# Delta stage on normed inputs, with its weight rests and masks on VectorE, in a kernel of six layers on one core

## The chip, the core and the metric

One core of a Trainium2 chip runs the whole program. TensorE (PE; its weight loads are PEld), VectorE (DVE), ScalarE (ACT), GpSimd (POOL) and SyncE (SP, which issues most transfers) each work through a queue of their own and meet by semaphores. The metric is the device time of one execution in microseconds; the median of the runs counts.

## What is computed

Six layers over x (512 tokens, 1024 channels), each with an RMS norm ahead and a residual behind: pooling, gated delta rule, latent attention, pooling, a state space layer with a depthwise convolution beside it, and differential attention. The change touches the delta rule's layer and the state space layer's begin:

```python
h = rmsnorm(x, norm_g)                       # x * rsqrt(mean(x*x) + EPS) * g
proj = h @ w_in
qkv, gate, b_raw, a_raw = jnp.split(proj, ...)
qkv = silu(causal_depthwise_conv(qkv, conv_w))        # 4 taps
q, k, v = jnp.split(qkv, [GDN_QK, 2 * GDN_QK], axis=-1)
...
L = strict lower part of (k_beta @ k.T) * decay
sol = solve_triangular(I + L, [v_beta, k_beta * exp(g)])
...
o = rmsnorm(o, norm_g) * silu(gate);  x = x + o @ w_out
```

and of the state space layer `u = glu_v * sigmoid(glu_g)`, then a causal convolution of 31 taps over u. It reads a norm of a norm: x is first scaled by the final norm of the first four layers.

## The kernel before

Activations lie with channels on the 128 partitions and the 512 tokens in the free dimension: x is eight blocks of 128x512. Every projection is done with three fp32r matmuls per 128 channels of the input (`mm3`, L285 to L290): weight and input are each split into a rounded part and a rest. One unit is a 128-column slab of weights, 128x1024: a transfer (L278), a cast `wh` on ScalarE (L281), a subtraction `wl` on the engine that `self.rest` names (L282), and 24 matmuls of 128x512 into one bank of PSUM. `self.rest` is VectorE, but GpSimd during the delta stage from the first head on (`gdn`, L821 to L829) and in the state space layer (`even`, from L1129).

The inputs of a projection are x times the gain, split by `split_scaled` (L264 to L269) into tiles of the group "h", while the stage before still writes x. The norm r (one number per token, in all partitions) comes later, and each unit's result is scaled by it when it leaves PSUM: in place by `scaled_psum` (L500) ahead of a convolution of four taps (ScalarE L550, VectorE three times L555), or into a tile by `scaled` (L495).

The delta stage, `gdn`: a small unit for the gates, eight units of keys (`k_unit`), of which the last four are woven with `k_chain` (for each head a row broadcast L603, the decays L612 and L615, the product of the keys L691, and its scaling L695); then five units for each of the eight heads (`head_units`), woven with the inverse of the triangular matrices (`inverse`: small products L876 and sums L877, then for each of three levels and four heads a mask L908, matmuls L915, a copy L917, matmuls and subtractions L902, L903), with the recurrence over four chunks (`rec`: L746, L769 to L786) and the norm of its output (L804, L805, split L260, L261).

The state space layer begins with `final_begin`: r of the sum of squares, and from it r2, the norm of the normed x (L1117 to L1120). x itself is scaled by the first norm, one block after each of eight units pairs (`final_x`, L1124), the units' results by r2 (L495). From the second pair on, the taps of the long convolution (L1161) are woven in, with accumulators in the bank "a".

The Tile framework takes the program in the order in which it is written and woven, as priorities, and from dependencies and free buffers fixes the order of each engine's queue when the kernel is built. Buffers come from groups of equal tiles and banks:

```python
TAGS = {"h": 16, "y": 36, "t": 8, "c": 6, "sq": 2, "r": 1, "rope": 3}
BANKS = {"mm": 3, "a": 2, "b": 2, "c": 1}
```

Of the kernel before, what the change touches and what calls it, by code (L numbers as in the profile page):

```python
# [14 lines left out]
ALU = mybir.AluOpType  # L15
# [4 lines left out]
P = 128  # L20
# [148 lines left out]

TAGS = {"h": 16, "y": 36, "t": 8, "c": 6, "sq": 2, "r": 1, "rope": 3}  # L170
BANKS = {"mm": 3, "a": 2, "b": 2, "c": 1}
# [24 lines left out]
class Net:  # L196
# [94 lines left out]

    def proj(self, slabs, h, kt, c=P):

        wv = [
            [w[:, : kt * c].rearrange("p (k c) -> p k c", k=kt) for w in self.load_w(s, kt * c)] for s in slabs
        ]
        nk = kt * len(slabs)
        m = min(c, P)
        out = []
        for j in range(max(c // P, 1)):  # L300
            ps = self.ps()
            for k in range(nk):
                hi, lo = wv[k // kt]
                sl = slice(j * m, j * m + m)
                self.mm3(ps[:m], (hi[:, k % kt, sl], lo[:, k % kt, sl]), h[k], k == 0, k == nk - 1)
            out.append(ps)
        return out
# [73 lines left out]
    def prep(self, i, g):  # L381

        return self.split_scaled(self.x[i], g, "h")

# [233 lines left out]

    def gdn(self, gnext):
        nc, a = self.nc, self.a  # L620
        r = self.norm_r()
        conv = lambda ct, u, tag: self.conv4(u, lambda k: self.p("gconv", k * 32 + ct), tag=tag)

        def conv_unit(ct, tag="t"):
            (ps,) = self.proj([a["gdn_in"][ct]], self.h, 8)
            return conv(ct, self.scaled_psum(ps, r), tag)

# [30 lines left out]
        def k_unit(hd):  # L658
            sil[hd] = conv_unit(8 + hd, "y")
            if hd % 4 == 3:  # L660
                self.silus([sil[i] for i in range(hd - 3, hd + 1)])
                for i in range(hd - 3, hd + 1):
                    sil[i] = sil[i][0]
# [43 lines left out]
        def head_units(hd):  # L707
            st = heads[hd] = {}

            items = []  # L710
# [4 lines left out]
            def gate(i):  # L715
                (ps,) = self.proj([a["gdn_in"][32 + hd * 2 + i]], self.h, 8)
                items.append((self.scaled(ps, r, "y"), self.last, {}))
                if i == 0:
                    return
                self.silus(items)  # L720
                st["q"], _, _, st["g0"], st["g1"] = [it[0] for it in items]
                st["v"] = [self.big("y", shape=[P, 2, 256]) for _ in range(2)]
                for k in range(2):
                    pt = self.transpose4(items[1 + k][0], "c")
                    for j in range(2):
                        nc.vector.tensor_tensor(
                            st["v"][j][:, :, k * P : k * P + P],
                            pt[:, j * 256 : j * 256 + 256].rearrange("p (c d) -> p c d", c=2),
                            sk[:, hd, 2 * j : 2 * j + 2].unsqueeze(2).to_broadcast([P, 2, P]), op=ALU.mult,
                        )  # L730
# [89 lines left out]
        recs = recs()  # L820
        self.rest = nc.gpsimd  # L821
        weave(head_units(0), (solve(0), 4), (k_chain(range(4, 8)), 2))
# [5 lines left out]
        early, rest = self.out_units(self.two_slabs("gdn_out"), y, gnext, ["mm"] * 3)  # L828
        self.rest = nc.vector  # L829
        weave(early, (recs, 99))  # L830
# [3 lines left out]
    def inverse(self, grp, mt, xt):  # L834
# [70 lines left out]
        for l in (1, 2, 3):  # L905
            for n, hd in enumerate(hs):
                ml = self.big("c")
                nc.gpsimd.tensor_tensor(  # L908
                    ml.rearrange("p (c d) -> p c d", c=4), mt[hd].rearrange("p (c d) -> p c d", c=4),
# [93 lines left out]
    def mla(self, gnext):  # L1003
# [39 lines left out]
        def units(hp, st):  # L1043
            def v(vg):
                if vg == 0:
                    state["v"] = [self.big("h") for _ in range(4)]
                vN = state["v"]
# [5 lines left out]
            def q(i):  # L1053
                (ps,) = self.proj([a["mla_uq"][hp * 3 + i]], cq, 6)
                t = self.big("t")
                nc.scalar.copy(t, ps)
                st["q"].append(self.stacked(self.rope(t, cos, sin, mask, "t"), "h") if i == 2 else t)

# [12 lines left out]
        def attend(hp, st, vN):  # L1071
            q, k = st["q"], st["k"]
            for i in range(2):
# [4 lines left out]
                for qb in range(NC):  # L1078
# [9 lines left out]
                    if prev is not None:  # L1088
                        self.weighted(*prev)
                    prev = (pr, qb, vh, po, "h")  # L1090
                    yield 1
# [19 lines left out]
    def final_begin(self):  # L1111
# [7 lines left out]
        r2 = self.norm_of(t, "rope")  # L1119
        nc.vector.tensor_tensor(r2, r2, r, op=ALU.mult)  # L1120
        return r, r2

    def final_x(self, i, r):
        self.nc.vector.scalar_tensor_tensor(  # L1124
            self.x[i], self.x[i], self.p("final", i), r, op0=ALU.mult, op1=ALU.mult
        )

    def even(self, gnext):
        nc, a = self.nc, self.a  # L1129
        rf, r = self.final_begin()  # L1130
        self.rest = nc.gpsimd
        W = lambda i: a["ssd_in"][i]
        u = []

        def plain(slab, tag="t"):
            (ps,) = self.proj([slab], self.h, 8)
            return self.scaled(ps, r, tag)
# [3 lines left out]
        def glu(t):  # L1141
            v = plain(W(24 + t), "y")
            z = plain(W(32 + t))
            nc.scalar.activation(z, z, AF.Tanh, scale=0.5)
# [35 lines left out]
        for t in range(8):  # L1180
            glu(t)
            if t:
                bg(8)
            self.final_x(t, rf)
        self.log_exp()
# [307 lines left out]
def body(tc, a, out, poff, coff, layers=LAYERS):  # L1493
    with ExitStack() as ctx:
# [9 lines left out]
        for n, l in enumerate(layers):  # L1504
# [3 lines left out]
            elif l[0] == "g":  # L1508
                net.gdn(g)
            elif l[0] == "m":  # L1510
# [25 lines left out]
```

## Time and profile before

| what | value |
| --- | --- |
| median of 3 runs | 2520.25 us (2518.78 to 2520.77) |
| the profiled execution's own time | 2517.89 us |
| its span, granted TensorE clock | 2516.1 us, 0.993 |
| busy, PE / PEld | 2447.9 / 1978.1 us |
| busy, DVE / ACT / POOL | 1578.2 / 1066.3 / 475.0 us |
| moved by DMA | 204.41 MB |

Busy shares of PE are of overlapping matmuls: a new one starts before the last one ends. What TensorE loses is seen in its idle time and in the granted clock (1.00 is the upper of its two levels, 2.4 GHz; 0.5 is 1.2 GHz). The delta stage lies from about 319 to 861 us, the state space layer from about 1730 us on. Idle time of an engine is put down to the instruction whose semaphore came last.

### The profile page before, as it was taken

What the parts mean: (1) busy time and instruction counts of PE and PEld (TensorE: products, weight loads), DVE (VectorE), ACT (ScalarE), POOL (GpSimd) and SP (SyncE); (2) the same over time, 40 slices, a digit from 0 to 9 for tenths busy, and PEclk for the clock granted to TensorE, in tenths of its full rate; (3) what the DMA queues carried; (4) which work ended last, traced back from release to release, by engine and by line L of the source; (5) the groups of instructions that cost most, each with busy time, mean ns of one, the idle gap of its engine ahead of it and who ended that gap; (6) DMA issues with size and microseconds to landing.
All of it is one profiled execution on the core that took longest, in us unless ns stands there. A gap on an engine that the chain in (4) does not pass through costs nothing.

```text
span 2516.1 us, 30894 instructions
## 1 busy us (share of the span) xinstructions
PE 2447.9 (97%) x11852; PEld 1978.1 (79%) x11852; DVE 1578.2 (63%) x2796; ACT 1066.3 (42%) x1684; POOL 475.0 (19%) x378
## 2 busy tenths in 40 slices
PE   8999999999999999999999999998999998999999
PEld 6888877877877878888878888887877776877777
DVE  6666367576465354356665466635998897468774
ACT  4323354344444343444454333333244555365553
POOL 0121103423320120000000111214344453100000
PEclk9999999999999999999999999999999999999999
DMA  4232324222112322311212323232222211321122
GB/s 155 94 101 92 97 78 140 82 57 86 51 49 70 104 84 92 97 47 61 64 53 76 98 95 101 92 101 84 85 84 68 68 59 59 99 67 60 59 66 78
DMA packets 73460, 204.41 MB, mean 81 GB/s; under 512 B 19904, under 2 KB 20032, under 8 KB 73312
## 3 DMA queue, kind: packets, MB, share of 16 engines
q1 hardware_dynamic: 72816, 200.91, 24.7%
q8 instruction: 94, 1.54, 0.2%
q10 hardware_dynamic: 288, 0.86, 0.1%
q0 software_dynamic: 208, 0.66, 0.1%
q14 instruction: 54, 0.44, 0.1%
HBM read 195.58 MB, written 6.82 MB: 80 GB/s over the span
## 4 chain that ended last, share of the span: by engine, by line
PE 85%; DVE 8%; ACT 3%; issue 2%; POOL 1%; DMA 0%; SPq 0%; ACTq 0%; DVEq 0%; POOLq 0%
PE psmm L288 23%; PE psmm L290 23%; PE psmm L289 23%; PE psc L998 2%; PE psa L1448 1%; PE psa L1082 1%; PE psb L994 1%; DVE psa L1161 1%; PE psb L896 1%; ACT wh L281 1%; PE psc L368 1%; PE psa L915 1%; PE psb L775 1%; POOL wl L282 1%; DVE c L805 1%
## 5 line engine op out<-in xcount | busy, mean ns | idle before, releaser
L281 ACT CAST wh<-wr 128x1024 fp32r<-128x1024 f32 (+3 forms) x366 | 377.0, 1031 | 779.5 <-PE psmm L289 598.4
L288 PE MATMUL psmm<-h,wh 128*128 128x512 f32 x1704 | 682.8, 401 | 15.9 <-ACT wh L281 8.6
L290 PE MATMUL psmm<-h,wl 128*128 128x512 f32 x1704 | 679.4, 399 | 0.0
L289 PE MATMUL psmm<-h,wh 128*128 128x512 f32 x1704 | 678.1, 398 | 0.0
L282 DVE TENSOR_TENSOR wl<-wr,wh 128x1024 fp32r<-128x1024 f32 (+2 forms) x270 | 321.9, 1192 | 189.5 <-ACT wh L281 187.2
L288 PEld LDWEIGHTS psmm<-h,wh 128*128 128x128 f32 x1704 | 321.6, 189 | 91.0 <-issue 16.8
L289 PE MATMUL psmm<-y,wh 128*128 128x512 f32 x976 | 383.4, 393 | 0.0
L288 PE MATMUL psmm<-y,wh 128*128 128x512 f32 x976 | 383.2, 393 | 0.0
L290 PEld LDWEIGHTS psmm<-h,wl 128*128 128x128 f32 x1704 | 321.0, 188 | 78.6 <-issue 11.4
L290 PE MATMUL psmm<-y,wl 128*128 128x512 f32 x976 | 382.2, 392 | 0.0
L289 PEld LDWEIGHTS psmm<-h,wh 128*128 128x128 f32 x1704 | 321.5, 189 | 71.2 <-issue 5.9
L282 POOL TENSOR_TENSOR wl<-wr,wh 128x1024 fp32r<-128x1024 f32 (+1 forms) x96 | 235.5, 2455 | 491.9 <-ACT wh L281 406.4
L354 POOL TENSOR_TENSOR sq<-sq,sq 128x512 f32<-128x512 f32 x36 | 64.5, 1792 | 831.7 <-ACT sq L356 831.7
L289 PEld LDWEIGHTS psmm<-y,wh 128*128 128x128 f32 x976 | 183.4, 188 | 36.9 <-issue 0.7
L288 PEld LDWEIGHTS psmm<-y,wh 128*128 128x128 f32 x976 | 183.4, 188 | 36.6 <-DVE psa L1161 0.2
L290 PEld LDWEIGHTS psmm<-y,wl 128*128 128x128 f32 x976 | 183.4, 188 | 36.6 <-issue 0.2
L1161 DVE SCALAR_TENSOR_TENSOR psa<-y,par,psa 128x506 f32<-128x506 f32 (+28 forms) x232 | 164.5, 730 | 3.9 <-ACT psa L1157 1.6
L483 DVE TENSOR_TENSOR x<-psmm,x 128x512 f32<-128x512 f32 x44 | 30.3, 691 | 140.4 <-PE psmm L290 140.4
L495 DVE TENSOR_TENSOR t<-psmm,r 128x512 f32<-128x512 f32 (+1 forms) x74 | 50.8, 688 | 101.4 <-PE psmm L290 101.3
L983 ACT ACTIVATE c<-psa,smx,qs 128x128 f32<-128x128 f32 (+3 forms) x128 | 78.9, 617 | 82.7 <-DVE smx L981 81.7
L555 DVE SCALAR_TENSOR_TENSOR t<-psmm,par,t 128x509 f32<-128x509 f32 (+2 forms) x120 | 88.7, 741 | 7.5 <-ACT t L550 5.1
L260 ACT CAST y<-c 128x512 fp32r<-128x512 f32 x60 | 37.1, 621 | 98.9 <-POOL c L531 68.9
(359 smaller groups left out, 3322.7 us busy)
## 6 DMA issues: line engine op xcount, KB each, us to landing
wr<-in_pool_in_dram SPq DMA_DIRECT2D x64, 512.0 KB, 3.7
wr<-in_gdn_in_dram SPq DMA_DIRECT2D x48, 512.0 KB, 3.7
wr<-in_ssd_in_dram SPq DMA_DIRECT2D x48, 512.0 KB, 3.7
wr<-in_pool_out_dram SPq DMA_DIRECT2D x32, 512.0 KB, 3.6
wr<-in_mla_in_dram SPq DMA_DIRECT2D x27, 512.0 KB, 3.7
wr<-in_dif_in_dram SPq DMA_DIRECT2D x24, 512.0 KB, 3.7
wr<-in_mla_uq_dram SPq DMA_DIRECT2D x24, 384.0 KB, 3.0
wr<-in_pool_grp_dram SPq DMA_DIRECT2D x16, 512.0 KB, 3.6
```

Of the source, the lines that this page charges most:

```text
L260: nc.scalar.copy(hi, src)
L281: nc.scalar.copy(hi[:, :f], raw[:, :f])
L282: self.rest.tensor_tensor(lo[:, :f], raw[:, :f], hi[:, :f].bitcast(F32), op=ALU.subtract)
L288: nc.tensor.matmul(ps, wh, xh, start=start, stop=False)
L289: nc.tensor.matmul(ps, wh, xl, start=False, stop=False)
L290: nc.tensor.matmul(ps, wl, xh, start=False, stop=stop)
L354: (eng or nc.gpsimd).tensor_tensor(acc[0], acc[0], acc[1], op=ALU.add)
L495: self.last = self.nc.vector.tensor_tensor(t[:n], ps[:n], r[:n], op=ALU.mult)
L555: self.last = nc.vector.scalar_tensor_tensor(t[:, s:], u[:, : S - s], w(k), t[:, s:], op0=ALU.mult, op1=ALU.add)
L983: nc.scalar.activation(pr[:, :n], ps[:, :n], AF.Exp, bias=st[:, 1:2], scale=scale, accum_out=st[:, 2:3])
L998: nc.tensor.matmul(po[:, qb * P : n], vN[kb], pT[:, kb * P : kb * P + P], start=kb == 0, stop=kb == qb)
L1161: nc.vector.scalar_tensor_tensor(out[:, s:], z[:, : S - s], dw(k), acc[:, s:], op0=ALU.mult, op1=ALU.add)
```

## The change

Four things change. The inputs' splits and some other tiles go from the group "h" (16) to the group "y", which has all 52. In `gdn` only the gates' unit and the units 0 to 2 of the keys take the raw inputs and are scaled in PSUM (unit 2 in the bank "a"); behind unit 2 each block of x is multiplied by gain and norm and split anew by `apply_norm` (L452, cast L260, rest L261), and every later unit takes these, so that its result needs no scaling: the taps read PSUM as it is, and the gates' results are copied by ScalarE (L721). `self.rest` stays VectorE in the whole delta stage, and the 24 masks of `inverse` are VectorE's as well. In `even` `self.rest` becomes GpSimd only behind the second pair of units, one unit each of the second and third pair takes the bank "b", and `final_x` waits by a dependency of its own for the last operation of r2.

```diff
-TAGS = {"h": 16, "y": 36, "t": 8, "c": 6, "sq": 2, "r": 1, "rope": 3}
+TAGS = {"y": 52, "t": 8, "c": 6, "sq": 2, "r": 1, "rope": 3}
...
-    def proj(self, slabs, h, kt, c=P):
+    def proj(self, slabs, h, kt, c=P, bank="mm"):
...
-            ps = self.ps()
+            ps = self.ps(bank)
...
-        return self.split_scaled(self.x[i], g, "h")
+        return self.split_scaled(self.x[i], g, "y")
...
-    def gdn(self, gnext):
+    def gdn(self, g, gnext):
...
-        def conv_unit(ct, tag="t"):
-            (ps,) = self.proj([a["gdn_in"][ct]], self.h, 8)
-            return conv(ct, self.scaled_psum(ps, r), tag)
+        def conv_unit(ct, tag="t", bank="mm", raw=False):
+            (ps,) = self.proj([a["gdn_in"][ct]], self.h, 8, bank=bank)
+            return conv(ct, self.scaled_psum(ps, r) if raw else ps, tag)
...
         def k_unit(hd):
-            sil[hd] = conv_unit(8 + hd, "y")
+            sil[hd] = conv_unit(8 + hd, "y", "a" if hd == 2 else "mm", hd < 3)
+            if hd == 2:
+
+                self.h = [self.apply_norm(self.x[i], g(i), r) for i in range(8)]
...
-                items.append((self.scaled(ps, r, "y"), self.last, {}))
+                z = self.big("y")
+                items.append((z, nc.scalar.copy(z, ps), {}))
...
-        self.rest = nc.gpsimd
         weave(head_units(0), (solve(0), 4), (k_chain(range(4, 8)), 2))
...
-        self.rest = nc.vector
         weave(early, (recs, 99))
...
                 ml = self.big("c")
-                nc.gpsimd.tensor_tensor(
+                nc.vector.tensor_tensor(
...
-        nc.vector.tensor_tensor(r2, r2, r, op=ALU.mult)
-        return r, r2
-
-    def final_x(self, i, r):
-        self.nc.vector.scalar_tensor_tensor(
+        return r, r2, nc.vector.tensor_tensor(r2, r2, r, op=ALU.mult)
+
+    def final_x(self, i, r, after):
+
+        op = self.nc.vector.scalar_tensor_tensor(
             self.x[i], self.x[i], self.p("final", i), r, op0=ALU.mult, op1=ALU.mult
         )
+        info = mybir.DependencyInfo(mybir.DependencyClass.Sync, mybir.DependencyReason.DATA)
+        self.tc.add_manual_dep(op.ins, after.ins.name, info, reason="the norm first")
...
-        rf, r = self.final_begin()
-        self.rest = nc.gpsimd
+        rf, r, last_r = self.final_begin()
...
-            v = plain(W(24 + t), "y")
-            z = plain(W(32 + t))
+
+            v = plain(W(24 + t), "y", "b" if t == 2 else "mm")
+            z = plain(W(32 + t), "t", "b" if t == 1 else "mm")
...
             glu(t)
+            if t == 1:
+                self.rest = nc.gpsimd
             if t:
                 bg(8)
-            self.final_x(t, rf)
+            self.final_x(t, rf, last_r)
```

After the change the line numbers of the recurrence are higher by four (L746 becomes L750), those of `inverse` by two. Left out of the diff are MLA's tiles that go from "h" to "y" and the argument g of `gdn`.

The order on VectorE at the end of the keys' unit 2, before. psmm_2549 is that unit's bank, y_2575 its convolution, and wl the rests of the next weights:

```order
L555 SCALAR_TENSOR_TENSOR y_2538<-psmm_2512,par,y_2538 128x511
L500 TENSOR_TENSOR psmm_2549<-psmm_2549,r_2379 128x512
L282 TENSOR_TENSOR wl_2681<-wr_2678,wh_2680 128x1024
L555 SCALAR_TENSOR_TENSOR y_2575<-psmm_2549,par,y_2575 128x509
L555 SCALAR_TENSOR_TENSOR y_2575<-psmm_2549,par,y_2575 128x510
L555 SCALAR_TENSOR_TENSOR y_2575<-psmm_2549,par,y_2575 128x511
L500 TENSOR_TENSOR psmm_2586<-psmm_2586,r_2379 128x512
L282 TENSOR_TENSOR wl_2755<-wr_2752,wh_2754 128x1024
L555 SCALAR_TENSOR_TENSOR y_2612<-psmm_2586,par,y_2612 128x509
L555 SCALAR_TENSOR_TENSOR y_2612<-psmm_2586,par,y_2612 128x510
L555 SCALAR_TENSOR_TENSOR y_2612<-psmm_2586,par,y_2612 128x511
```

And after the change, from the same scaling on (psa_2549 is the same bank; y_2583, y_2589 and so on are the rests of the normed inputs, c_2580 to c_2622 the products ahead of them):

```order
L500 TENSOR_TENSOR psa_2549<-psa_2549,r_2379 128x512
L282 TENSOR_TENSOR wl_2672<-wr_2669,wh_2671 128x1024
L555 SCALAR_TENSOR_TENSOR y_2575<-psa_2549,par,y_2575 128x509
L261 TENSOR_TENSOR y_2583<-c_2580,y_2582 128x512
L555 SCALAR_TENSOR_TENSOR y_2575<-psa_2549,par,y_2575 128x510
L261 TENSOR_TENSOR y_2589<-c_2586,y_2588 128x512
L555 SCALAR_TENSOR_TENSOR y_2575<-psa_2549,par,y_2575 128x511
L261 TENSOR_TENSOR y_2595<-c_2592,y_2594 128x512
L452 SCALAR_TENSOR_TENSOR c_2616<-x_80,par,r_2379 128x512
L261 TENSOR_TENSOR y_2601<-c_2598,y_2600 128x512
L452 SCALAR_TENSOR_TENSOR c_2622<-x_81,par,r_2379 128x512
L261 TENSOR_TENSOR y_2607<-c_2604,y_2606 128x512
```

The scaling of units 3 (psmm_2586) is gone, and six rests of the normed inputs and two more products stand among the taps.

TensorE's order at the second to fourth pair of key products, before (psa_2857 is such a product, psa_2867 a row broadcast, psmm_2891 a head's unit):

```order
L289 MATMUL psmm_2891<-h_1886,wh_2887 128x512
L290 MATMUL psmm_2891<-h_1885,wl_2888 128x512
L288 MATMUL psmm_2891<-h_1953,wh_2887 128x512
L289 MATMUL psmm_2891<-h_1954,wh_2887 128x512
L691 MATMUL psa_2857<-y_2575 128x128 x4
L603 MATMUL psa_2867<-rope_2455,sel 128x512
L290 MATMUL psmm_2891<-h_1953,wl_2888 128x512
L288 MATMUL psmm_2891<-h_2021,wh_2887 128x512
L289 MATMUL psmm_2891<-h_2022,wh_2887 128x512
L290 MATMUL psmm_2891<-h_2021,wl_2888 128x512
L288 MATMUL psmm_2891<-h_2090,wh_2887 128x512
```

And after, at the same product (psa_2900; psmm_2865 is the keys' last unit, psmm_2934 and psmm_3022 are the first head's):

```order
L694 MATMUL psa_2841<-y_2538 128x128 x4
L603 MATMUL psa_2851<-rope_2455,sel 128x512
L289 MATMUL psmm_2865<-y_2625,wh_2861 128x512
L290 MATMUL psmm_2865<-y_2624,wl_2862 128x512
L288 MATMUL psmm_2934<-y_2582,wh_2930 128x512
L289 MATMUL psmm_2934<-y_2583,wh_2930 128x512
L288 MATMUL psmm_3022<-y_2582,wh_3018 128x512
L289 MATMUL psmm_3022<-y_2583,wh_3018 128x512
L694 MATMUL psa_2900<-y_2575 128x128 x4
L603 MATMUL psa_2910<-rope_2455,sel 128x512
L694 MATMUL psa_2918<-y_2659 128x128 x4
L603 MATMUL psa_3129<-rope_2455,sel 128x512
```

Three products and three broadcasts stand close together, with six projection matmuls between them.

VectorE's order at the state space layer's begin, before (rope_13395 becomes r2, c_13393 the norm's square, x_74 to x_81 are the blocks of x):

```order
L1117 TENSOR_TENSOR c_13390<-r_13381 128x512
L1124 SCALAR_TENSOR_TENSOR x_74<-x_74,par,r_13381 128x512
L1118 TENSOR_TENSOR c_13390<-psc_13388,c_13390 128x512
L1124 SCALAR_TENSOR_TENSOR x_75<-x_75,par,r_13381 128x512
L409 TENSOR_SCALAR c_13393<-c_13390 128x512
L1124 SCALAR_TENSOR_TENSOR x_76<-x_76,par,r_13381 128x512
L399 TENSOR_TENSOR c_13393<-c_13393,rope_13395 128x512
L1124 SCALAR_TENSOR_TENSOR x_77<-x_77,par,r_13381 128x512
L400 TENSOR_TENSOR c_13393<-c_13393,rope_13395 128x512
L1124 SCALAR_TENSOR_TENSOR x_78<-x_78,par,r_13381 128x512
L401 SCALAR_TENSOR_TENSOR rope_13395<-c_13393,rope_13395 128x512
L1124 SCALAR_TENSOR_TENSOR x_79<-x_79,par,r_13381 128x512
```

And after, where r2 is rope_13414:

```order
L282 TENSOR_TENSOR wl_13527<-wr_13524,wh_13526 128x1024
L401 SCALAR_TENSOR_TENSOR r_13400<-c_13398,r_13400 128x512
L1119 TENSOR_TENSOR c_13409<-r_13400 128x512
L1120 TENSOR_TENSOR c_13409<-psc_13407,c_13409 128x512
L409 TENSOR_SCALAR c_13412<-c_13409 128x512
L596 MEMSET rope_14103 128x512
L399 TENSOR_TENSOR c_13412<-c_13412,rope_13414 128x512
L400 TENSOR_TENSOR c_13412<-c_13412,rope_13414 128x512
L401 SCALAR_TENSOR_TENSOR rope_13414<-c_13412,rope_13414 128x512
L1122 TENSOR_TENSOR rope_13414<-rope_13414,r_13400 128x512
L495 TENSOR_TENSOR y_13453<-psmm_13428,rope_13414 128x512
L495 TENSOR_TENSOR t_13486<-psmm_13461,rope_13414 128x512
```

The scalings of x (L1124, now L1126) stand behind r2 and the first two results that need it, and a weight rest stands ahead.

## Rows read from the trace of the kernel before

**Rows 1.** Part 1 of the page: busy us, share of the span, instructions.
```profile
PE 2447.9 (97%) x11852; PEld 1978.1 (79%) x11852; DVE 1578.2 (63%) x2796; ACT 1066.3 (42%) x1684; POOL 475.0 (19%) x378
```

**Rows 2.** Busy us by stretch: length, PE, PEld, DVE, ACT, POOL; PEclk, DMA share, GB/s.
```profile
319.00:391.00 72.00, 71.59 (x350) 57.27 (x349) 51.93 (x101) 41.66 (x59) 7.66 (x4) 1.00 0.33 111
391.00:428.00 37.00, 31.64 (x163) 26.44 (x162) 31.19 (x79) 16.09 (x23) 13.80 (x10) 0.95 0.35 103
480.00:620.00 140.00, 131.41 (x651) 103.83 (x650) 93.32 (x167) 65.28 (x97) 40.51 (x22) 1.00 0.26 75
620.00:720.00 100.00, 94.50 (x562) 80.70 (x561) 54.64 (x87) 39.52 (x58) 34.04 (x19) 1.00 0.13 43
720.00:861.00 141.00, 140.39 (x658) 111.92 (x657) 72.72 (x108) 59.18 (x84) 18.76 (x9) 1.00 0.23 75
1719.00:1765.00 46.00, 38.66 (x155) 30.30 (x154) 30.96 (x34) 17.39 (x22) 18.97 (x8) 0.93 0.22 69
1765.00:2085.00 320.00, 308.44 (x1462) 245.26 (x1461) 288.17 (x433) 146.12 (x247) 150.22 (x100) 0.99 0.22 73
```

**Rows 3.** Waits of PE, 319 to 861: us in total, times, longest.
```profile
PE psb L775 <- DVE c L612: 6.5, 4, 1.8
PE psa L603 <- DVE c L612: 4.1, 1, 4.1
PE psb L775 <- DVE q L771: 2.9, 2, 1.7
PE psa L915 <- POOL c L908: 2.2, 2, 1.7
```

**Rows 4.** Timeline of DVE, 486 to 502: start us, us, line, operation [idle before].
```profile
497.62 0.18 DVE L876 TENSOR_TENSOR y<-y,y 128x16 f32<-128x16 f32 x1
...
498.84 2.21 DVE L876 TENSOR_TENSOR y<-y,y 128x25 f32<-128x25 f32 x1
```

**Rows 5.** Timeline of POOL, 484 to 512.
```profile
498.60 2.40 POOL L282 TENSOR_TENSOR wl<-wr,wh 128x1024 fp32r<-128x1024 f32 x1 [6.62 <-ACT wh L281]
```

**Rows 6.** Groups by form, DVE, 319 to 861: busy us, mean ns | idle before.
```profile
L282 DVE TENSOR_TENSOR wl<-wr,wh 128x1024 fp32r<-128x1024 f32 x23 | 28.1, 1222 | 16.5 <-ACT wh L281 16.5
...
L805 DVE TENSOR_TENSOR c<-c,y 128x512 f32<-128x512 f32 x16 | 19.8, 1277 | 0.0
...
L268 DVE SCALAR_TENSOR_TENSOR h<-x,par,h 128x512 fp32r<-128x512 f32 x7 | 5.2, 746 | 0.0
```

**Rows 7.** Groups by form, POOL, 319 to 861.
```profile
L282 POOL TENSOR_TENSOR wl<-wr,wh 128x1024 fp32r<-128x1024 f32 x40 | 95.5, 2389 | 302.5 <-ACT wh L281 228.3 <-DVE ssq L432 55.3 <-PE psmm L290 6.6
L908 POOL TENSOR_TENSOR c<-y,con 128x512 f32<-128x512 f32 x24 | 32.2, 1357 | 12.5 <-PE psb L901 12.5
```

**Rows 8.** Groups by form, ACT, 319 to 861.
```profile
L260 ACT CAST y<-c 128x512 fp32r<-128x512 f32 x16 | 9.8, 622 | 17.2 <-DVE c L805 17.1
```

**Rows 9.** Timeline of DVE, 319 to 349.
```profile
328.57 0.68 DVE L401 SCALAR_TENSOR_TENSOR r<-c,r 128x512 f32<-128x512 f32 x1
...
345.48 0.69 DVE L500 TENSOR_TENSOR psmm<-psmm,r 128x512 f32<-128x512 f32 x1
```

**Rows 10.** Waits of PE, 1719 to 1765.
```profile
PE psmm L288 <- DVE y L495: 5.7, 1, 5.7
PE psc L368 <- DVE sq L363: 1.6, 1, 1.6
```

**Rows 11.** Timeline of DVE, 1730 to 1757.
```profile
1731.76 2.36 DVE L268 SCALAR_TENSOR_TENSOR h<-x,gfa,h 128x512 fp32r<-128x512 f32 x1 [0.83 <-ACT h L267]
...
1740.22 0.69 DVE L1117 TENSOR_TENSOR c<-r 128x512 f32<-128x512 f32 x1
...
1751.84 2.82 DVE L1120 TENSOR_TENSOR rope<-rope,r 128x512 f32<-128x512 f32 x1
```

**Rows 12.** Waits of PE, 1760 to 2110.
```profile
PE psc L1337 <- ACT y L1165: 2.6, 1, 2.6
```

More of the change, by code (lines that the diff above doesn't have):

```diff
@@ L1045, in v @@
                 if vg == 0:
-                    state["v"] = [self.big("h") for _ in range(4)]
+                    state["v"] = [self.big("y") for _ in range(4)]
                 vN = state["v"]
@@ L1056, in q @@
                 nc.scalar.copy(t, ps)
-                st["q"].append(self.stacked(self.rope(t, cos, sin, mask, "t"), "h") if i == 2 else t)
+                st["q"].append(self.stacked(self.rope(t, cos, sin, mask, "t"), "y") if i == 2 else t)
             def k():
@@ L1089, in attend @@
                         self.weighted(*prev)
-                    prev = (pr, qb, vh, po, "h")
+                    prev = (pr, qb, vh, po, "y")
                     yield 1
@@ L1119, in final_begin, with plain @@
         r2 = self.norm_of(t, "rope")
-        nc.vector.tensor_tensor(r2, r2, r, op=ALU.mult)
-        return r, r2
-    def final_x(self, i, r):
-        self.nc.vector.scalar_tensor_tensor(
+        return r, r2, nc.vector.tensor_tensor(r2, r2, r, op=ALU.mult)
+    def final_x(self, i, r, after):
+        op = self.nc.vector.scalar_tensor_tensor(
             self.x[i], self.x[i], self.p("final", i), r, op0=ALU.mult, op1=ALU.mult
         )
+        info = mybir.DependencyInfo(mybir.DependencyClass.Sync, mybir.DependencyReason.DATA)
+        self.tc.add_manual_dep(op.ins, after.ins.name, info, reason="the norm first")
     def even(self, gnext):
         nc, a = self.nc, self.a
-        rf, r = self.final_begin()
-        self.rest = nc.gpsimd
+        rf, r, last_r = self.final_begin()
         W = lambda i: a["ssd_in"][i]
         u = []
-        def plain(slab, tag="t"):
-            (ps,) = self.proj([slab], self.h, 8)
+        def plain(slab, tag="t", bank="mm"):
+            (ps,) = self.proj([slab], self.h, 8, bank=bank)
             return self.scaled(ps, r, tag)
@@ L1508, in body @@
             elif l[0] == "g":
-                net.gdn(g)
+                net.gdn(gains[l], g)
             elif l[0] == "m":
```

## The prediction

> **What bounds the kernel now.** I read the page's busy shares first: TensorE is busy for 97% of the span [rows 1], so the time can only fall where TensorE stands still or runs at its lower clock. Second, the table by stretch for the delta stage (319 to 861 us) and the state space layer's begin [rows 2]: a stretch's length less its PE time is what TensorE lost. From 391 to 428 that is 37.00 - 31.64 = 5.4 us, from 480 to 620 8.6, from 620 to 720 5.5, from 720 to 861 0.6, but from 319 to 391 only 0.4. The layer's begin, 1719 to 1765, loses 46.00 - 38.66 = 7.3, and its granted clock was 0.93, a further 0.07 x 46 = 3.2 us; in 391 to 428 it was 0.95, or 1.9 us. Third, PE's waits in the delta stage [rows 3]: nearly all end on VectorE (L612, L771) or on a GpSimd mask (L908). Fourth, why VectorE was late, from its timeline and GpSimd's [rows 4, 5]: the product L876 of 128x16 took 0.18 us, the next one, of 128x25, 2.21 us, and that one ran beside GpSimd's weight rest (498.60 to 501.00). A VectorE operation with both inputs in SBUF stands still while GpSimd's tensor operation runs. L805 shows it in the mean, 1277 ns for 128x512 where L268 takes 746 [rows 6]. So GpSimd's 40 rests and 24 masks [rows 7] cost VectorE more than their absence would suggest, and the queue behind the blocked operation is late for TensorE.
>
> **What the change does to each engine.** In the delta stage 40 rests go from GpSimd (95.5 us there) to VectorE: 40 x 1.222 = +48.9 us [rows 6, 7]. 24 masks (32.2 us on GpSimd) follow at about 0.69 us each, near L500's 694 ns: +16.5. New are 8 norm products (746 ns, as L268) and 8 subtractions (0.69): +11.5. Gone are 29 scalings at 0.694 (L500) and 16 gate scalings at about the same: -31.2. What stood still beside GpSimd comes back: L805 alone 16 x (1277 - 694) = 9.3 us; with the others I put it at 20. VectorE's sum is about +26 us. In the five stretches of this stage that the rows show it was busy 303.8 of 490 us, 62%, so the sum isn't a bound; where it falls is. ScalarE gains 8 casts and 16 copies, 24 x 0.62 = +15 us [rows 8], on an engine busy for 42 of 72 and 65 of 140 us there [rows 2]; I cost it at nothing but for the one cast in the chain below. TensorE's matmuls are the same, two rows regrouped. SP issues the same weight transfers in the same order. GpSimd's queue loses what stood behind its rests, the masks: that wait goes with them.
>
> **Begin of the delta stage, +3.5 us.** Up to unit 2 of the keys, projections use raw inputs. The norm r is ready at 329.2 [rows 9], and 8 products have to fit behind it, between the taps of units 0 and 1, into VectorE's idle time (20 of 72 us in this stretch). The order of the change puts the first lower part (L261) behind unit 2's scaling, a rest and a tap. That scaling ran at 345.48 to 346.17 [rows 9]; 1.22 + 0.75 + 0.69 later, at 348.8, the first lower part exists, and TensorE has only two matmuls without it: 3.3 us, where nothing was lost before. Units 3 and 4 then run interleaved, six matmuls for each part. Six take 6 x 71.59/350 = 1.2 us by the stretch's mean, and VectorE needs 0.69 + 0.75 for one part and the tap or product beside it: nearly in step, 0.2 more. Bounds: 1.5, if the casts come early and part of unit 2's end hides it; 8, if a rest (1.22) enters twice and the clock falls as after 1750, where it took 3.2.
>
> **First decay products, +5 us.** In the change's order three pairs of key product and row broadcast (L694, L603) stand on TensorE with six projection matmuls between them, where the order before has 7 to 15 between two pairs; the next projection waits for a rest that VectorE does behind the eight decays (L612) and kk products. The nearest row is the wait of L603 for L612, 4.1 us for one [rows 3]; with half a clock stretch 5. Bounds 0 (VectorE, relieved, is early) and 8 (two such waits).
>
> **391 to 428, -6 us.** The 4.1 us wait [rows 3] and the rest of the 5.4 us come from VectorE work held up by GpSimd's rests and a mask. They go, and the 1.9 us of clock: -7.2 at most; a rest on VectorE in the same place gives some back. Bounds -7.2 and 0, for VectorE is busy 31.19 of 37 us here, the fullest place of the stage.
>
> **428 to 861, -7.4 us.** 8.6 + 5.5 + 0.6 = 14.7 us were lost. L908's 2.2 us go with the mask's queue. L775's waits for L612 and L771 [rows 3] stem from blocked operations, except one of four that I can't put down to GpSimd (6.5/4 = 1.6 stay). New: in heads 4, 6 and 7 a rest lands before the query's product (L750 after the change), 1.22 + 0.69 = 1.9 each, 5.7 us, late for the same L775. 14.7 - 1.6 - 5.7 = 7.4. Bounds: -14.7, and +2 if every head gets such a rest (8 x 1.9 + 1.6 - 14.7).
>
> **State space layer's begin, -8.5 us.** L268 (2.36 us, blocked by GpSimd's rest) goes back to 0.74: the wait of 1.6 us [rows 10] goes. The norm's chain from L1117 (1740.22) to the end of L1120 (1754.66) [rows 11] has the final scalings between its steps, and L1120 alone took 2.82 blocked. Without either it is seven operations at 0.69 or less and ScalarE's two at about 0.62, some 6 us, with one rest of 1.22 ahead: r2 at about 1745.5 to 1748. TensorE wanted it at about 1750 (the wait of 5.7 us [rows 10] ended one result behind L1120's end), and two more banks put that off. The 5.7 us wait and 3.2 us of clock go: -10.5. Given back: 4 rests (4.9 us) and the final scalings come later on VectorE, whose last taps of the long convolution end with TensorE waiting 2.6 us [rows 12]. VectorE has 320 - 288.17 = 32 us of idle time before that [rows 2], so I take 2. Bounds -10.5 and -4.
>
> **One group of buffers, +0.5 us** (-1 to +4): no instruction comes or goes; at MLA's end a few splits come later, in a stage that TensorE fills.
>
> **Sum:** 3.5 + 5 - 6 - 7.4 - 8.5 + 0.5 = -12.9 on the profiled execution's 2517.89 us: 2505.0. The median is 2.4 above that execution, so 2507 for the median of the runs.
>
> **A rule against it.** VectorE is at 84% in the fullest stretch [rows 2] and gets more work there. The Trainium skill's page Perfetto Trace Analysis, section Optimizing Scalar/DVE Operations, says that with a saturated VectorE "offloading some work to Scalar (or even GPSIMD) may make sense", and this change goes the other way; by that rule the stage gets slower, as in the slow rival below. The same section adds that moving work between these two might not help since they share a port; the blocked L876 agrees with that half.
>
> **Rivals.**
> - *Cover holds (0.18).* The begin's 8.5 us hide behind work that I counted as late, and the -14.7 bound is nearly reached: -22, 2498. For it: VectorE's relief is at the very products that TensorE waits for. Against: only two matmuls can run without a lower part.
> - *The delta stage gives nothing (0.17).* Its four terms cancel, and only the state space layer's begin remains: -8.5 + 0.5, 2512. For it: the new waits are of the kind of the old.
> - *The long convolution's tail takes it back (0.12),* or buffers in one group make the scheduler lose at MLA's end: the change doesn't do what it says at that layer. Delta -5, layer -2, MLA +4: 2517, no change that can be told.
> - *VectorE becomes the bound (0.11), slower.* The point from which it decides is added work above VectorE's idle time just where TensorE waits: 37 - 31.2 = 5.8 us are idle in 391 to 428, and GpSimd's 13.8 us there are some 7 at VectorE's price (1.222 for 2.389), so it decides unless the unblocked products give back 1.3 or more. Begin +8, products +8, nothing back in 391 to 428, +2 later, less 8 for the layer: +10, 2530.
>
> **How the numbers follow.** The forecast has 0.42. Some 5 us (0.2%) can be told from no change. Faster: 0.42 + 0.18 + most of the second rival, 0.15, gives 0.75. Same: 0.12 + 0.02 = 0.14. Slower 0.11. The range 2495 to 2519 leaves out the slow rival and the far ends of the others, the bounds of the terms in it.
>
> **What would show it.** Right: L876, L805 and L750 lose their 2 us instances; TensorE's gaps in 391 to 428 and in 1719 to 1765 go, with granted clock 1.00; a new gap of some 3 us stands at 345 to 349 ahead of the first L289 of unit 3, waiting for L261, and one at the kk pairs, waiting for L612 or L282. Wrong: no gap at 345 (first term), or gaps of 2 us in every head that end on L282 or L750 (the slow rival), or a wait at the long convolution's end of over 5 us.

## The result and the profile after

The changed kernel takes 2494.52 us in the median (2493.05 to 2495.28) where the kernel before takes 2520.41: the ratio is 0.9897, 95% interval 0.9885 to 0.9909, some 26 us less where 13 were forecast (2507), and just below the range's end of 2495. The profiled execution's span falls by 23.4 us, from 2516.1 to 2492.7; the other 2.5 come from the kernel before, whose profiled execution was that much below its median, while the changed kernel's was at its median.

Where it came from is read from the ends of the stages, by VectorE's first or last addition to x (L483) in each. The first of the delta stage's end comes at 797.4 instead of 810.5: -13.1. The last of MLA's comes at 1717.4 instead of 1730.2, so MLA gave back 0.3. The last of the state space layer's comes at 2164.9 instead of 2188.3: another -10.6 in that layer. The rest is unchanged.

The stretches of the changed kernel (length, PE, PEld, DVE, ACT, POOL, then granted clock, DMA share, GB/s) answer to [rows 2]; the last one is the state space layer's begin, 13 us earlier than before:

```profile
319.00:391.00 72.00, 65.49 (x310) 51.12 (x309) 55.34 (x108) 42.15 (x62) 1.00 (x4) 0.96 0.25 84
391.00:428.00 37.00, 37.00 (x188) 31.32 (x188) 29.24 (x82) 15.96 (x23) 0.66 (x4) 0.98 0.43 129
...
480.00:620.00 140.00, 139.11 (x710) 111.97 (x709) 95.70 (x176) 69.11 (x105) 0.14 (x1) 1.00 0.25 75
620.00:720.00 100.00, 99.64 (x579) 84.32 (x578) 58.96 (x96) 42.43 (x64) 0.00 (x0) 1.00 0.17 53
720.00:861.00 141.00, 140.69 (x654) 113.30 (x653) 70.93 (x102) 61.25 (x87) 11.73 (x7) 1.00 0.25 78
1706.00:1752.00 46.00, 46.00 (x200) 36.97 (x199) 35.35 (x43) 19.69 (x25) 10.95 (x6) 1.00 0.24 81
```

Nothing is idle in 391 to 428 any more, and from 480 to 861 some 1.6 us are, where 14.7 were; but 319 to 391 has lost 72 - 65.49 = 6.5, against 0.4, at a clock of 0.96. The waits of PE in the delta stage (total, times, longest) answer to [rows 3], of which none is left:

```profile
PE psa L694 <- DVE y L698: 3.0, 2, 2.8
PE psmm L288 <- ACT y L260: 2.4, 1, 2.4
...
PE psb L773 <- DVE q L790: 0.5, 1, 0.5
PE psmm L289 <- DVE y L261: 0.4, 1, 0.4
```

And the groups on VectorE (busy, mean ns | idle before) show that these products no longer stand still: L809, the L805 of before, takes 683 ns in place of 1277, and L750, the L746 of before, 686; the longest L878, the L876 of before, takes 0.61 us in place of 2.21. It does 63 rests where it did 23.

```profile
L282 DVE TENSOR_TENSOR wl<-wr,wh 128x1024 fp32r<-128x1024 f32 x63 | 76.9, 1222 | 56.6 <-ACT wh L281 54.9 <-PE psmm L290 1.6
...
L809 DVE TENSOR_TENSOR c<-c,y 128x512 f32<-128x512 f32 x16 | 10.3, 683 | 0.0
...
L750 DVE TENSOR_TENSOR c<-t,c 128x512 f32<-128x512 f32 x8 | 5.5, 686 | 1.4 <-ACT t L339 1.4
```

### The profile page after: what moved, and what is told of

Its sections match the earlier page's. It is cut to its first block, busy times and chain, and to the rows that moved or that the text cites. A ratio compares the mean times of both kernels' runs of the same rounds, so it can differ in the third digit from the quotient of the medians.

```text
span 2492.7 us, 30840 instructions
## 1 busy us (share of the span) xinstructions
PE 2443.6 (98%) x11852; PEld 1976.8 (79%) x11852; DVE 1586.8 (64%) x2835; ACT 1077.4 (43%) x1708; POOL 336.8 (14%) x310
## 4 chain that ended last, share of the span: by engine, by line
PE 84%; DVE 9%; ACT 3%; issue 2%; POOL 1%; DMA 1%; SPq 0%; ACTq 0%; DVEq 0%; POOLq 0%
PE psmm L288 22%; PE psmm L290 22%; PE psmm L289 22%; DVE psa L1165 3%; PE psc L1000 2%; PE psa L1454 1%; PE psa L1084 1%; PE psb L996 1%; PE psb L898 1%; PE psa L917 1%; PE psc L368 1%; ACT wh L281 1%; PE psb L779 1%; PE psb L903 1%; DVE wl L282 1%
## 5 line engine op out<-in xcount | busy, mean ns | idle before, releaser
L288 PE MATMUL psmm<-y,wh 128*128 128x512 f32 x2656 | 1054.1, 397 | 12.7 <-ACT wh L281 8.5
L289 PE MATMUL psmm<-y,wh 128*128 128x512 f32 x2656 | 1053.7, 397 | 0.4 <-DVE y L261 0.4
L290 PE MATMUL psmm<-y,wl 128*128 128x512 f32 x2656 | 1052.7, 396 | 0.0
L288 PEld LDWEIGHTS psmm<-y,wh 128*128 128x128 f32 x2656 | 500.0, 188 | 124.3 <-issue 11.1
L290 PEld LDWEIGHTS psmm<-y,wl 128*128 128x128 f32 x2656 | 500.0, 188 | 113.5 <-issue 11.5
L289 PEld LDWEIGHTS psmm<-y,wh 128*128 128x128 f32 x2656 | 499.9, 188 | 107.2 <-issue 5.9
L282 DVE TENSOR_TENSOR wl<-wr,wh 128x1024 fp32r<-128x1024 f32 (+2 forms) x314 | 375.6, 1197 | 234.4 <-ACT wh L281 230.9
L1165 DVE SCALAR_TENSOR_TENSOR psa<-y,par,psa 128x495 f32<-128x495 f32 (+28 forms) x232 | 164.6, 732 | 2.9 <-ACT psa L1161 0.8
L282 POOL TENSOR_TENSOR wl<-wr,wh 128x1024 fp32r<-128x1024 f32 (+1 forms) x52 | 129.0, 2483 | 182.4 <-ACT wh L281 175.3
L483 DVE TENSOR_TENSOR x<-psmm,x 128x512 f32<-128x512 f32 x44 | 30.3, 691 | 136.6 <-PE psmm L290 136.6
L495 DVE TENSOR_TENSOR t<-psmm,r 128x512 f32<-128x512 f32 (+1 forms) x74 | 50.8, 688 | 101.5 <-PE psmm L290 101.3
L260 ACT CAST y<-c 128x512 fp32r<-128x512 f32 x68 | 41.5, 620 | 92.6 <-POOL c L531 68.6
L1000 PEld LDWEIGHTS psc<-y,y 128*128 128x128 f32 x480 | 63.3, 192 | 21.8 <-ACT y L998 11.0
L1000 PE MATMUL psc<-y,y 128*128 128x128 f32 x480 | 73.4, 284 | 3.4 <-ACT y L998 2.9
L288 PE MATMUL psmm<-wh,y 128*128 128x256 f32 x256 | 74.3, 290 | 0.0
L289 PE MATMUL psmm<-wl,y 128*128 128x256 f32 x256 | 73.7, 288 | 0.0
L290 PE MATMUL psmm<-wh,y 128*128 128x256 f32 x256 | 73.6, 288 | 0.0
```

The source lines that it names most:

```text
L282: self.rest.tensor_tensor(lo[:, :f], raw[:, :f], hi[:, :f].bitcast(F32), op=ALU.subtract)
L288: nc.tensor.matmul(ps, wh, xh, start=start, stop=False)
L289: nc.tensor.matmul(ps, wh, xl, start=False, stop=False)
L290: nc.tensor.matmul(ps, wl, xh, start=False, stop=stop)
L495: self.last = self.nc.vector.tensor_tensor(t[:n], ps[:n], r[:n], op=ALU.mult)
L1000: nc.tensor.matmul(po[:, qb * P : n], vN[kb], pT[:, kb * P : kb * P + P], start=kb == 0, stop=kb == qb)
```

## Experiments

All are edits of the changed kernel, unless another is named, and are compared with the kernel before on the same chip.

**1. Without the normed inputs.** Every unit takes the raw inputs and is scaled in PSUM; rests and masks stay on VectorE.

```diff
-        def conv_unit(ct, tag="t", bank="mm", raw=False):
+        def conv_unit(ct, tag="t", bank="mm", raw=True):
...
-            sil[hd] = conv_unit(8 + hd, "y", "a" if hd == 2 else "mm", hd < 3)
+            sil[hd] = conv_unit(8 + hd, "y", "mm", True)
-            if hd == 2:
-                self.h = [self.apply_norm(self.x[i], g(i), r) for i in range(8)]
...
-                z = self.big("y")
-                items.append((z, nc.scalar.copy(z, ps), {}))
+                items.append((self.scaled(ps, r, "y"), self.last, {}))
```

> The changed kernel with every unit of the delta stage on raw inputs and scaled out of PSUM again; the rests and masks stay on VectorE. Theory 1 (the gain of the heads comes from GpSimd no longer blocking VectorE; the normed inputs only cost at the begin): the gaps at 345 and 386 us go (2.4 + 0.4 + 2.8 us and two half-clock stretches of 1.7 us), the heads keep nearly all of their gain: 2486 to 2496. Theory 2 (the heads gain because units leave PSUM without a scaling; VectorE would be too full with the rests and the scalings): the heads lose again, 2502 to 2512.

2490.69 us, ratio 0.9886 (0.9869 to 0.9902): theory 1. The normed inputs bring nothing where the rests are on VectorE; the interval overlaps that of the whole change, so whether they cost a little can't be told. The wait at 345 is gone with them. The wait for the key products is not, so my reading, that the order of the normed inputs made it, does not hold:

```profile
PE psa L691 <- DVE y L695: 2.8, 1, 2.8
...
PE psa L603 <- DVE c L612: 0.4, 1, 0.4
```

**2. Rests and masks on GpSimd again.**

```diff
         recs = recs()
+        self.rest = nc.gpsimd
...
+        self.rest = nc.vector
         weave(early, (recs, 99))
...
-                nc.vector.tensor_tensor(
+                nc.gpsimd.tensor_tensor(
                     ml.rearrange("p (c d) -> p c d", c=4), mt[hd]...
```

> The changed kernel with the 40 rests and 24 masks of the delta stage on GpSimd again, normed inputs kept. Theory 1: VectorE's products are blocked again, L876 and L805 with 2 us instances, most of the 14 us of idle time between 428 and 861 come back: 2504 to 2512. Theory 2: the heads stay as they are: 2492 to 2498.

2514.63 us, 0.9985 (0.9974 to 0.9996): 0.0088 or 22 us are lost, somewhat more than theory 1 asked for. What is left of the gain, some 4 us, is less than the state space layer's 11 (experiment 3), so the delta stage is some 7 us slower here than in the kernel before. In the profiled execution it ends 10.7 us later (its first L483 at 821.2), but that execution was the longest of ten. So beside GpSimd's rests the normed inputs do cost; the one group of buffers doesn't (experiment 4), and unit 2's bank was not tried apart.

**3. The state space layer as before,** that is, without the diff's lines from `final_begin` on.

> The changed kernel with the state space layer's begin as it was (rests on GpSimd from its first unit, final scalings between the steps of r2, banks of one group). If the 10.6 us that the trace shows there belong to this part alone: 2504 to 2506, with waits of 1.6 and 5.7 us at its begin. If part of it came from the time shift of the stage before: 2498 to 2502.

2504.49 us, 0.9941 (0.9927 to 0.9956): 11 us of the gain are gone, the layer's part alone. Its waits are 1.6 and 5.7 us, as in [rows 10].

**4. One group of buffers alone,** in the kernel before.

> The kernel before with one group of 52 buffers in place of 16 and 36, nothing else. Theory 1 and 2: no change, 2518 to 2522. Rival 3 (the room in the group lets VectorE and ScalarE run ahead, and part of the gain is its): 2505 to 2516.

2519.67 us, 1.0005 (0.9996 to 1.0015): no change.

**5 and 6. Only the rests, or only the masks, on GpSimd,** one edit of the second experiment each.

> The changed kernel with only the 40 rests of the delta stage on GpSimd again; masks on VectorE. If the rests' 95 us of GpSimd work block VectorE's products: most of the 20 us that rests and masks cost together, 2507 to 2513, with waits of L779 for L612 and L775. If the queue of masks behind rests was the larger part: 2498 to 2502.

> The changed kernel with only the 24 masks on GpSimd again; rests on VectorE. The masks' own share is the waits for L908 and L917 (2.2 + 1.3 us) and the splits that stand beside them: 2496 to 2501 by the blocking of VectorE; 2494 to 2496 if masks harm only when they queue behind rests.

The rests: 2515.63 us, 0.9979 (0.9970 to 0.9988), 2.6 us above what I expected and the whole loss of experiment 2. The masks: 2493.62 us, 0.9894 (0.9879 to 0.9908), none. With the masks PE's longest waits are those of the changed kernel (L694 3.0 us in all, L288 2.4). With the rests old waits are back (L779 is the L775 of before), and the wait of 2.8 us for the key products (L694) has gone down to 0.3:

```profile
PE psb L779 <- DVE c L612: 4.3, 3, 1.7
PE psa L603 <- DVE c L612: 3.9, 1, 3.9
PE psb L779 <- DVE q L775: 3.3, 2, 1.7
```

So masks on GpSimd cost nothing where the rests are on VectorE, and no wait of PE ends on one. That they were late in the kernel before (L915 in [rows 3]) because they queued behind rests fits this, but is not shown by itself: beside the rests they added nothing to the loss either.

**7. GpSimd does rests that nobody reads.** The 40 rests stay on VectorE and are done once more on GpSimd, so nothing reads GpSimd's result. Two things are added: GpSimd is busy, and a weight's buffer comes free only when GpSimd has read it too.

```diff
         self.rest.tensor_tensor(lo[:, :f], raw[:, :f], hi[:, :f].bitcast(F32), op=ALU.subtract)
+        if self.idle:
+            d = self.wp.tile([P, 1024], F32, tag="dum", name=f"dum{n}", bufs=1)
+            nc.gpsimd.tensor_tensor(d[:, :f], raw[:, :f], hi[:, :f].bitcast(F32), op=ALU.subtract)
```

> The changed kernel, rests and masks on VectorE, and for each of the 40 rests the same subtraction once more on GpSimd, into a tile that nobody reads (the group has 50 buffers in place of 52 to make room; the result is the same). If VectorE's standing still beside GpSimd is the cause, the loss comes back though nothing waits for GpSimd: 2505 to 2516, with 2 us instances of L750, L809 and L878. If GpSimd's lateness was the cause: 2493 to 2497.

2517.20 us, 0.9990 (0.9980 to 0.9999): 0.0093 or 23 us are lost, as much as with the real rests on GpSimd, and no wait of PE ends on GpSimd. The groups on GpSimd and VectorE and the waits of PE (line numbers are three higher: L812 is L809, L753 is L750, L782 is L779):

```profile
L285 POOL TENSOR_TENSOR dum<-wr,wh 128x1024 f32<-128x1024 f32 x40 | 119.7, 2993 | 330.0 <-ACT wh L281 304.8 <-issue 25.1
```

```profile
L812 DVE TENSOR_TENSOR c<-c,y 128x512 f32<-128x512 f32 x16 | 12.9, 845 | 0.0
...
L753 DVE TENSOR_TENSOR c<-t,c 128x512 f32<-128x512 f32 x8 | 10.5, 1307 | 1.4 <-ACT t L342 1.4
```

```profile
PE psa L697 <- DVE y L701: 8.3, 5, 3.2
...
PE psb L782 <- DVE c L615: 2.0, 1, 2.0
...
PE psb L782 <- DVE q L778: 1.2, 1, 1.2
```

GpSimd's own subtraction is slowed too, 2993 ns against 2389 in [rows 7]: it stands still for VectorE as well. VectorE is busy for 367.0 us with the same 617 operations that take it 340.8 in the changed kernel. PE's waits end on VectorE's scaling of the key products (L701; the 2.8 us that the changed kernel has are among the 8.3), its decays (L615) and the recurrence (L778). The longest, of 3.2 us at 421.76, comes behind a product of 128x64 on VectorE that takes 0.27 us elsewhere and here ends as GpSimd's subtraction does, with no idle time on VectorE from there to the wait's end:

```profile
414.00 2.11 DVE L883 TENSOR_TENSOR y<-y,y 128x64 f32<-128x64 f32 x1
```

```profile
413.57 2.41 POOL L285 TENSOR_TENSOR dum<-wr,wh 128x1024 f32<-128x1024 f32 x1 [3.22 <-ACT wh L281]
```

The buffers are the rival: weight transfers wait 41.6 us in all for the unread subtractions, and casts 13.1 us for transfers in place of 3.4. But of PE's waits only 0.4 us end on a weight's rest and none on a weight's cast. Another 4.0 us have no releaser in the profile. So VectorE's standing still beside GpSimd brings the loss back without GpSimd's result being late for anything.

**8. Two more operations ahead of the query's product.** They tell whether a delay of the prediction's size harms there.

```diff
+            d = self.small([P, 512], "dum", 1)
+            for _ in range(2):
+                nc.vector.tensor_tensor(d, q, qe, op=ALU.mult)
             nc.vector.tensor_tensor(qe, q, qe, op=ALU.mult)
```

> The changed kernel with two more products of 0.69 us on VectorE ahead of the query's product in each of the eight heads, between its exponential and it, into a tile that nobody reads (51 buffers in place of 52). By the step of the prediction (an operation ahead of that product makes TensorE late by its length): 8 x 1.4 = +11, 2503 to 2508. By the theory that the order, which is fixed with knowledge of these operations, moves projection matmuls ahead of the waiting ones (35 in place of 27 in the second head, 17 in place of 11 in the fifth) and that only unforeseen lengths are felt: 2494 to 2498.

2495.04 us, 0.9898 (0.9883 to 0.9912): no loss that can be told, where the prediction's step asks for 11. Sixteen operations (L752) stand where the prediction put its price, and PE's longest waits are those of the changed kernel (L694 3.0 us, L288 2.4):

```profile
L752 DVE TENSOR_TENSOR dum<-t,c 128x512 f32<-128x512 f32 x16 | 10.9, 684 | 0.3 <-ACT t L339 0.2
...
L753 DVE TENSOR_TENSOR c<-t,c 128x512 f32<-128x512 f32 x8 | 5.4, 681 | 0.0
```

**9. The parts of the state space layer's begin.** First only the rests on VectorE, with the dependency and the second bank taken out; then only these, with the rests on GpSimd.

```diff
-        self.tc.add_manual_dep(op.ins, after.ins.name, info, reason="the norm first")
...
-            v = plain(W(24 + t), "y", "b" if t == 2 else "mm")
-            z = plain(W(32 + t), "t", "b" if t == 1 else "mm")
+            v = plain(W(24 + t), "y", "mm")
+            z = plain(W(32 + t), "t", "mm")
```

> The changed kernel with only the rests of the state space layer's first two pairs on VectorE: no dependency that holds the final scalings back, no second bank. Theory (blocked operations made the begin late: 6.4 us in two scalings and L1120, 1.6 in L268): the scalings cost 0.74 each in the chain, r2 is ready just in time, 2494 to 2498. If the scalings' place in the queue was the cause: 2499 to 2504.

> The changed kernel with the state space layer's rests on GpSimd from its first unit, the final scalings held back and the second bank kept. By the same theory L268 stays blocked (1.6 us) and one or two of r2's steps may be; without the scalings r2 still comes before TensorE needs it: 2495 to 2498. If the place of the rests alone decides: 2501 to 2505.

Rests alone: 2501.83 us, 0.9929 (0.9914 to 0.9943), against my theory; a wait of 6.4 us for L495 is back. Order and bank alone: 2495.10 us, 0.9901 (0.9886 to 0.9916), all of the layer's gain but a wait of 1.6 us. Here the place of the final scalings in the queue decides, more than the blocking. The wait that each version has, rests alone first:

```profile
PE psmm L288 <- DVE y L495: 6.4, 1, 6.4
```

```profile
PE psc L368 <- DVE sq L363: 1.6, 1, 1.6
```

VectorE's timeline of the changed kernel, then of rests alone:

```profile
1727.30 0.69 DVE L1119 TENSOR_TENSOR c<-r 128x512 f32<-128x512 f32 x1
...
1731.63 2.77 DVE L401 SCALAR_TENSOR_TENSOR rope<-c,rope 128x512 f32<-128x512 f32 x1
1734.44 0.69 DVE L1122 TENSOR_TENSOR rope<-rope,r 128x512 f32<-128x512 f32 x1
1735.16 0.69 DVE L495 TENSOR_TENSOR y<-psmm,rope 128x512 f32<-128x512 f32 x1
```

```profile
1726.95 0.69 DVE L1119 TENSOR_TENSOR c<-r 128x512 f32<-128x512 f32 x1
...
1729.82 4.21 DVE L1126 SCALAR_TENSOR_TENSOR x<-x,par,r 128x512 f32<-128x512 f32 x3
...
1736.49 2.82 DVE L401 SCALAR_TENSOR_TENSOR rope<-c,rope 128x512 f32<-128x512 f32 x1
...
1739.90 0.68 DVE L1122 TENSOR_TENSOR rope<-rope,r 128x512 f32<-128x512 f32 x1
```

From the start of L1119 to the start of L1122 it takes 7.1 us in the one and 12.95 in the other, where eight scalings (L1126) stand between, one of them blocked: three take 4.21, 3 x 0.74 would be 2.2. So of the 5.8 us some 2 are blocking and the rest is the scalings' place. One step of r2 is blocked in both (2.77 and 2.82), so the change did not end that here. The bank by itself was not tried, but the traces bound it: with rests alone TensorE stopped at 1735.4 and waited until 1741.8, and in the changed kernel the first result (L495) has left its bank at 1735.9. With the scalings held back and no second bank it would have waited for about half a microsecond, an estimate from these times.

**10. A version that beats both.** Experiment 1, and the last of the seven early rests at the state space layer's end on VectorE: it took 7.59 us on GpSimd beside VectorE's operations, and TensorE waited for it.

```diff
-        for f in early:
-            f()
+        for f in early[:-1]:
+            f()
         self.rest = nc.vector
+        early[-1]()
```

```profile
2101.30 7.59 POOL L282 TENSOR_TENSOR wl<-wr,wh 128x1024 fp32r<-128x1024 f32 x1 [20.63 <-ACT wh L281]
```

```profile
PE psb L290 <- POOL wl L282: 4.5, 1, 4.5
PE psc L1343 <- ACT y L1169: 2.6, 1, 2.6
```

> The kernel with all units scaled out of PSUM (as in the first experiment) and, at the state space layer's end, the seventh of the seven early weight rests on VectorE in place of GpSimd, where it took 7.6 us in the changed kernel and TensorE waited 4.5 us for it. If that wait has nothing behind it: 2484 to 2487. If the next rest or split takes its place: 2488 to 2492.

2484.79 us, 0.9859 (0.9842 to 0.9876). In its waits of PE in the same stretch the other row alone is left:

```profile
PE psc L1339 <- ACT y L1165: 2.6, 1, 2.6
```

## Why the prediction was wrong

**The begin of the delta stage (+3.5) was right in size, not in its wait.** It came to 4.5: TensorE stood still for 2.40 and 0.42 us where I had 3.3, and a half-clock stretch of 3.4 us behind that cost another 1.7. The first lower part started at 347.83 on VectorE, where I had worked it out, but only the 0.42 waited for it. The 2.40 waited for the cast of the upper part (L260), which stood in ScalarE's queue behind unit 2's first tap (L550), and that behind unit 2's scaling. I had costed ScalarE at nothing but for one cast; the size came out because both ways start at the same scaling. VectorE's rows first, then ScalarE's and PE's:

```profile
345.44 0.69 DVE L500 TENSOR_TENSOR psa<-psa,r 128x512 f32<-128x512 f32 x1
...
347.83 0.68 DVE L261 TENSOR_TENSOR y<-c,y 128x512 fp32r<-128x512 f32 x1
```

```profile
346.17 0.69 ACT L550 ACTIVATE y<-psa,par 128x512 f32<-128x512 f32 x1 [3.96 <-DVE psa L500]
346.75 1.13 ACT L260 CAST y<-c 128x512 fp32r<-128x512 f32 x2
```

```profile
347.41 0.73 PE L288 MATMUL psmm<-y,wh 128*128 128x512 f32 x2 [2.40 <-ACT y L260]
348.57 0.80 PE L289 MATMUL psmm<-y,wh 128*128 128x512 f32 x1 [0.42 <-DVE y L261]
```

**The key products (+5) were right in size:** 3.0 us of waits, the longest 2.79, and 1.7 of clock. The wait was for the products' scaling (L698), not for L612 or L282. It stays without the normed inputs (experiment 1) and goes with the rests back on GpSimd (experiment 5), so it comes from the rests on VectorE, not from the order that the normed inputs bring.

**391 to 428 (-6) was right:** 5.4 us of idle time and the 1.9 of clock are gone, all of the 7.2 that I had as the bound. The clock of 0.98 that is left is the end of the key products' half-clock stretch, counted there.

**428 to 861 (-7.4) was the step that failed.** It came to -13.1 - 4.5 - 4.7 + 7.2 = -15.1, past its bound of -14.7, which counted idle time alone. I let 5.7 us of new waits stand ("in heads 4, 6 and 7 a rest lands before the query's product, 1.22 + 0.69 = 1.9 each, late for the same L775") and 1.6 that I couldn't put down to GpSimd. Neither is in the trace: from 428 on the idle time fell from 14.7 to 1.9, and the remaining 2.3 us of this stretch's gain I can't put to a row. Why the 1.6 went too stays open: of the four waits for L612, three are back with the rests on GpSimd (experiment 5). For the 5.7, the fifth head (number 4) shows why; in heads 6 and 7, the seventh and eighth, the query's product came behind the decays and waited for ScalarE, not for a rest. Before, in the fifth head, on VectorE and then PE, the blocked product:

```profile
677.13 2.54 DVE L746 TENSOR_TENSOR c<-t,c 128x512 f32<-128x512 f32 x1 [0.63 <-ACT c L745]
```

```profile
680.85 0.67 PE L775 MATMUL psb<-y,y 128*128 128x256 f32 x2 [1.74 <-DVE c L612]
```

And after, with the rest ahead of it as foreseen:

```profile
668.28 1.22 DVE L282 TENSOR_TENSOR wl<-wr,wh 128x1024 fp32r<-128x1024 f32 x1 [4.28 <-ACT wh L281]
669.42 0.68 DVE L750 TENSOR_TENSOR c<-t,c 128x512 f32<-128x512 f32 x1
670.03 1.12 DVE L612 SCALAR_TENSOR_TENSOR c<-psb,cs,con 128x128 f32<-128x128 f32 x4
```

```profile
671.29 0.67 PE L779 MATMUL psb<-y,y 128*128 128x256 f32 x2
```

From the head's row broadcast (675.53 and 667.19) the product started 1.6 us later before and 2.2 after: the rest ran while ScalarE's exponential was still at work, and delayed it by 0.6, not by 1.9. And TensorE arrives at L779 after 11 projection matmuls in place of 8: the order, fixed when the kernel is built, had put more work ahead of a wait that it could foresee. A blocked operation is longer than the order knows, and nothing has been put there to cover it.

Experiment 8 adds 1.4 us of foreseen work at all eight places and costs nothing that can be told, with 35 in place of 27 projection matmuls ahead in the second head and 17 in place of 11 in the fifth. Was there slack anyway? In the changed kernel TensorE reaches L779 4 to 6 us after the decays' end in the fourth, seventh and eighth head; there it was slack. In the other five it comes 0.1 to 0.8 us after them, too little for 1.4 us more, and in experiment 8 it still doesn't wait: there the order's filling covered the delay. The fifth head of experiment 8, the last decays on VectorE and then the product (L782 is L779), where 11 matmuls would have brought TensorE 1.4 us earlier:

```profile
671.66 0.60 DVE L612 SCALAR_TENSOR_TENSOR c<-psb,cs,con 128x128 f32<-128x128 f32 x2
```

```profile
672.60 0.59 PE L782 MATMUL psb<-y,y 128*128 128x256 f32 x2
```

Experiment 7 adds no work that TensorE needs and costs 23 us, more than the 13 that the delta stage had gained.

**The state space layer's begin (-8.5) was mis-sized by 2:** -10.6. The wait of 1.6 + 5.7 us and the clock went as worked out; the 2 us that I gave back at the long convolution's end didn't come, where TensorE waits 2.6 us as before. VectorE still has 30 us of idle time in the 320 us ahead of it, which I take to have held the rests. But the cause that I gave half of it to, the blocked operations, is worth only 1.6 us once the scalings are out of the chain (experiment 9).

**One group (+0.5):** 0.3 in the trace, and none in experiment 4. The terms as measured add up to the 23.4 us of the span. The rest of the miss is the 2.4 that I added for the median: that the changed kernel's profiled execution lay at its median was chance.

**The rivals.** The cover that held was the likeliest miss, though not at the begin where I put it. Its price was wrong in itself: -22 has only the 8.5 us of the begin in it; with the -14.7 that it names it would have been about -29, and the range's end of 2495 too high for it. VectorE did not become the bound: it is busy for 29.24 of 37 us in its fullest stretch of the delta stage, where it had 31.19. Its sum came to +12 us in place of +26 (309.1 us up to the stage's first L483 before, 320.9 after), so some 34 us rather than 20 must have stood still, if the other terms hold. The Trainium skill's page SBUF — State Buffer, section Who interferes with whom, says that VectorE and GpSimd share a pair of SBUF ports, and that it is an exclusive lock, not a division of bandwidth. Experiment 7 agrees: both engines' operations get longer (1307 for 686 ns in the mean, 2993 for 2389), and the product at 414.00 ends with GpSimd's subtraction.

## What to carry to other kernels

Count what an engine's operation does to the other engine's, not only its own time: here 95 us of rests on GpSimd cost some 13 us of the delta stage in the kernel that had them (experiment 1, whose stage ends 12.9 us earlier) and 21 in the changed one (experiment 5), and VectorE took them over, 49 us of work, without TensorE waiting for it but at one place. A delay that the static order can foresee is not the same as one that it can't; price the first by what is not covered, and expect the second to be felt. And when a change comes in parts, try each alone: the most elaborate part here, the normed inputs, brought nothing.

## What I had not expected

The standing still goes both ways, and for a single operation GpSimd's share of it can be the larger: an unread rest took 2993 ns in the mean in place of 2389, and one rest at the state space layer's end 7.59 us, beside VectorE's subtractions, while the longest of VectorE's products L753 in experiment 7 took 2.88 us in place of 0.69. And a wait of a few microseconds cost TensorE more than its length: the waits of 2.4 and 2.8 us at 345 and 386 were each followed by 3.4 us at a granted clock of 0.5.
